# Alternating the products of two heads on TensorE, with shared PSUM tiles, in the four attentions of a two-layer block

## The chip, the cores and the metric

The kernel runs on one core of a Trainium2 chip. The metric is the device time of one execution in microseconds (us); a run of the kernel is a few such executions, and the median of them counts. A difference under 0.2% (about 2.2 us) can't be told from no change by such a measurement.

## The reference

Two transformer blocks over one sequence of 256 tokens, width 1024, all in float32. The first block has three branches that read the same normalised input: a pooling mixer, a stick-breaking attention with 8 heads of 64, and a cross attention with 4 heads of 64 over 256 memory rows. Their results are gated, merged, projected, and followed by a dense feed-forward layer. The second block has two causal attentions with 8 heads of 64 each (one of them with a top-64 selection of keys by an index score), gates, a projection, and a mixture of 32 experts with two experts per token.

```
# stick-breaking, per head:   z = q k^T / 8;  a = exp(logsig(z) + exclusive reverse cumsum(log1m));  out = a v
# cross, per head:            out = softmax(xq mk^T / 8) mv
# second block, per head:     out_a = softmax(causal(q k^T / 8)) v
#                             out_b = softmax(causal and top-64 by index score (q k^T / 8)) v
# then:  x = x + (sigmoid(ga) * (out_a w_a) + sigmoid(gb) * (out_b w_b)) w_out;   x = x + experts(x)
```

So there are four attentions: the stick-breaking one, the cross attention, and `attend` twice. In each of them the heads are worked through in pairs: 4 pairs, 2 pairs, and 4 pairs in each call of `attend`.

## The kernel before

Weights come from HBM as chunks of 1 MB on SyncE's queue, into rings of buffers. A chunk is split into a high part (ScalarE, L178, tiles `whi` or `wsw`) and a low part (VectorE, L179, `wlo` or `wsw`), and each dense product is three matmuls (`mm3`, L215 to L217). Dense products thus keep TensorE, ScalarE and VectorE busy together. The expert weights of the second block are used as they come.

The text of the kernel is not the order of the program. A list scheduler orders the instructions of each engine by its own estimate of when they are ready, and only `tc.issue_after` binds an order by hand. Around the attentions the dense products of the gates (tile `gate`) stand between the attention's products on TensorE, as filling.

Two heads of a pair lie on partitions 0 to 63 and 64 to 127. A score product contracts over 64 partitions, so head 0 uses the upper half of the array's rows and head 1 the lower half (shown as 64*128 in the trace). An output product contracts over all 128 and writes 64 partitions, so head 0 uses one half of the columns and head 1 the other (128*64). Every product in float32 appears as two matmul records.

The places that the change and the prediction touch:

- Stick-breaking (L534 to L565): scores `z` (L539, L541) into one tile of two PSUM banks, one bank per head; output `sbo` (L564).
- Cross attention (L570 on): scores `xs` (L576) into two tiles of one bank from the tag `m`; softmax; transposes `xpt` (L595) into another `m` tile per head; a copy `xpts` per head (L598, ScalarE); output `xob` (L605).
- `attend`, called for `b` and for `a` (L850 on): scores `as` (L860) into two tiles of one bank; maxima (L867, VectorE); exponentials (L874, ScalarE); reciprocal and scaling (L876, L880); three transposes per head back into the score's bank (L884); a copy `apts` per head (L886, ScalarE); output `ao` (L893).
- `acc_tile` hands out either a tile of two banks (pool `accp`, the first block up to the merge) or two tiles of one bank (pool `acc1`, four buffers, everything after). `ts_pair` uses it for the dense products with 512 columns: the two banks hold the two halves of the tokens. In the second block these are, in order, `qiT`, `qTb`, `kTb`, `vb`, `qTa`, `kTa`, `va`, ahead of `attend`'s score tiles.

What follows the attentions: the merge, the projection `wo2`, the routing, and eight groups of four experts, whose weights (201 MB) stream in on the same queue.

Of the kernel before, what the change touches and what calls it, by code (L numbers as in the profile page):

```python
# [18 lines left out]
P = 128  # L19
S = 256  # L20
# [61 lines left out]
def block_kernel(ctx: ExitStack, tc: tile.TileContext, A, out: bass.AP):  # L82
# [26 lines left out]
    def m_tile(n):  # L109
        return psum.tile([P, 512], F32, name=n, tag="m", bufs=2)  # L110
# [95 lines left out]
    def piece(v, a, b, after=(), eng=None):  # L206
        hi, lo = piece_tiles(a, b)
        with ExitStack() as q:
            for ins in after:
                q.enter_context(tc.issue_after(ins.ins))  # L210
            split_to(hi, lo, v, eng)
        return hi, lo

    def mm3(o, lh, rh, start, stop):
        nc.tensor.matmul(o, lhsT=lh[0], rhs=rh[0], start=start, stop=False)  # L215
# [318 lines left out]
    for hp in range(4):  # L534
        z = acc_tile("z")[2]
        zv = z[:, :, :384]
        for j in range(2):
            ks = slice(j * 64, j * 64 + 64)
            nc.tensor.matmul(z[:, j, 0:256], lhsT=kT[ks, hp, 0:P], rhs=qT[ks, hp, :], start=True, stop=True,  # L539
                             skip_group_check=True)  # L540
            nc.tensor.matmul(z[:, j, 256:384], lhsT=kT[ks, hp, P:S], rhs=qT[ks, hp, P:S], start=False, stop=True,  # L541
                             skip_group_check=True)
        e = tmp.tile([P, 2, 384], F32, name="se", tag="se", bufs=3)
        nc.scalar.activation(e, zv, AF.Abs)
        nc.scalar.activation(e, e, AF.Exp, scale=-1.0)
        nc.scalar.activation(e, e, AF.Ln, bias=1.0)
        nc.vector.scalar_tensor_tensor(out=e, in0=zv, scalar=0.0, in1=e, op0=ALU.max, op1=ALU.add)
        nc.vector.tensor_tensor(out=e, in0=e, in1=keep[:, None, :].to_broadcast([P, 2, 384]), op=ALU.mult)
        for j in range(2):
            nc.tensor.matmul(z[:, j, 0:256], lhsT=cst("tri"), rhs=e[:, j, 0:256], start=False, stop=True,  # L550
                             skip_group_check=True)
            nc.tensor.matmul(z[:, j, 128:256], lhsT=cst("one"), rhs=e[:, j, 256:384], start=False, stop=True,
                             skip_group_check=True)
            nc.tensor.matmul(z[:, j, 256:384], lhsT=cst("tri"), rhs=e[:, j, 256:384], start=False, stop=True,
                             skip_group_check=True)
        nc.vector.scalar_tensor_tensor(out=e, in0=zv, scalar=0.0, in1=drop[:, None, :].to_broadcast([P, 2, 384]),
                                       op0=ALU.min, op1=ALU.add)
        last_exp = nc.scalar.activation(e, e, AF.Exp)
        ob = m_tile("sbo")
        for k, c0, c1, a0 in ((0, 0, 256, 0), (1, 128, 256, 256)):  # L560
            for j in range(2):
                ps = slice(j * 64, j * 64 + 64)
                hc = slice((2 * hp + j) * 64, (2 * hp + j + 1) * 64)
                nc.tensor.matmul(ob[ps, c0:c1], lhsT=v[:, k, hc], rhs=e[:, j, a0:a0 + c1 - c0], start=(k == 0),  # L564
                                 stop=(k == 1), skip_group_check=True)  # L565
        split_to(sb[0][:, hp, :], sb[1][:, hp, :], ob[:, :S])


    xo = (mg1.tile([P, 2, S], F32R, name="xoh"), mg1.tile([P, 2, S], F32R, name="xol"))
    for hp in range(2):  # L570
        pts = []
        scs = [m_tile("xs").rearrange("p (t k) -> p t k", t=2) for j in range(2)]
        for tt in range(NT):
            for j in range(2):
                ks = slice(j * 64, j * 64 + 64)
                nc.tensor.matmul(scs[j][:, tt, :], lhsT=xqT[ks, hp, tt * P:(tt + 1) * P], rhs=mkT[ks, hp, :],  # L576
                                 start=True, stop=True, skip_group_check=True)
        for j in range(2):
            sc = scs[j]
            mx = tmp.tile([P, 2], F32, name="xmx", tag="xmx")  # L580
            nc.vector.tensor_reduce(out=mx, in_=sc, axis=AX.X, op=ALU.max, negate=True)
            pr = tmp.tile([P, 2, 256], F32, name="xp", tag="xp")
            sm = tmp.tile([P, 2], F32, name="xsm", tag="xsm")
            for tt in range(NT):
                nc.scalar.activation(pr[:, tt, :], sc[:, tt, :], AF.Exp, bias=mx[:, tt:tt + 1],
                                     accum_out=sm[:, tt:tt + 1])
            rc = tmp.tile([P, 2], F32, name="xrc", tag="xrc")
            nc.vector.reciprocal(rc, sm)
            for tt in range(NT):
                nc.vector.tensor_scalar(out=pr[:, tt, :], in0=pr[:, tt, :], scalar1=rc[:, tt:tt + 1],  # L590
                                        scalar2=None, op0=ALU.mult)
            pb = m_tile("xpt")
            for kt in range(2):
                for tt in range(NT):
                    nc.tensor.transpose(pb[:, kt * S + tt * P:kt * S + (tt + 1) * P],  # L595
                                        pr[:, tt, kt * P:(kt + 1) * P], ident)
            pt = tmp.tile([P, 2, S], F32, name="xpts", tag="xpts")
            nc.scalar.activation(pt.rearrange("p a s -> p (a s)"), pb, AF.Copy)  # L598
            pts.append(pt)
        ob = m_tile("xob")  # L600
        for kt in range(2):
            for j in range(2):
                ps = slice(j * 64, j * 64 + 64)
                hc = slice((2 * hp + j) * 64, (2 * hp + j + 1) * 64)
                nc.tensor.matmul(ob[ps, :S], lhsT=mv[:, kt, hc], rhs=pts[j][:, kt, :], start=(kt == 0),  # L605
                                 stop=(kt == 1), skip_group_check=True)
        split_to(xo[0][:, hp, :], xo[1][:, hp, :], ob[:, :S])


# [51 lines left out]

    ast.close()
    accp = None
    acc1 = ctx.enter_context(tc.tile_pool(name="acc1", bufs=4, space=PSUM, reuse_waits="tile"))
    accs = [acc_tile("wo") for _ in range(NT)]
    project("w_out", accs)
    s1.close()
# [121 lines left out]
        return dst  # L789


    qiT = rope_heads(3072, 1.0, "qiT", at, 4, first[0], 2)
    s1.close()
    homes.update(list=[base], i=0)
# [55 lines left out]
    def attend(qT, kT, v, bias, name):  # L850
        oh = (mg2.tile([P, 4, S], F32R, name=name + "h"), mg2.tile([P, 4, S], F32R, name=name + "l"))
        for hp in range(4):
            sc = acc_tile("as")
            st = tmp.tile([P, 16], F32, name="ast", tag="ast")
            mx, nm, sm, rc = (st[:, 4 * i:4 * i + 4] for i in range(4))
            prs, pts = [], []
            for j in range(2):
                ks = slice(j * 64, j * 64 + 64)
                for tt, a0, a1 in SPANS:
                    nc.tensor.matmul(sc[j][:, a0:a1], lhsT=qT[ks, hp, tt * P:(tt + 1) * P],  # L860
                                     rhs=kT[ks, hp, 0:a1 - a0], start=True, stop=True, skip_group_check=True)
            for j in range(2):
                pr = tmp.tile([P, 384], F32, name="ap", tag="ap", bufs=4)
                prs.append(pr)
                for tt, a0, a1 in SPANS:
                    c = 2 * j + tt
                    nc.vector.tensor_tensor_reduce(out=pr[:, a0:a1], in0=sc[j][:, a0:a1], in1=bias[:, a0:a1],  # L867
                                                   scale=1.0, scalar=GONE, op0=ALU.add, op1=ALU.max,
                                                   accum_out=mx[:, c:c + 1])
            nc.vector.tensor_scalar(out=nm, in0=mx, scalar1=-1.0, scalar2=None, op0=ALU.mult)  # L870
# [6 lines left out]
            for j in range(2):  # L877
                for tt, a0, a1 in SPANS:
                    c = 2 * j + tt
                    nc.vector.tensor_scalar(out=prs[j][:, a0:a1], in0=prs[j][:, a0:a1], scalar1=rc[:, c:c + 1],  # L880
                                            scalar2=None, op0=ALU.mult)
                pb = sc[j]
                for c in range(3):
                    nc.tensor.transpose(pb[:, c * P:(c + 1) * P], prs[j][:, c * P:(c + 1) * P], ident)  # L884
                pt = tmp.tile([P, 384], F32, name="apts", tag="apts")
                nc.scalar.activation(pt, pb[:, :384], AF.Copy)  # L886
                pts.append(pt)
            ob = m_tile("ao")
            for k, c0, c1, a0 in ((0, 0, 256, 0), (1, 128, 256, 256)):
                for j in range(2):  # L890
                    ps = slice(j * 64, j * 64 + 64)
                    hc = slice((2 * hp + j) * 64, (2 * hp + j + 1) * 64)
                    nc.tensor.matmul(ob[ps, c0:c1], lhsT=v[:, k, hc], rhs=pts[j][:, a0:a0 + c1 - c0], start=(k == 0),  # L893
                                     stop=(k == 1), skip_group_check=True)
            split_to(oh[0][:, hp, :], oh[1][:, hp, :], ob[:, :S])
        return oh

# [42 lines left out]
    for hf in range(2):  # L940
# [5 lines left out]
          for n, c in (("g", 1), ("s", 1), ("t", 1), ("u", 1), ("o", 2))}  # L946
    rings = [sw, (mgp, 2), (r3["g"], 1), (r3["s"], 1), (ring2r, 1), (ring2b, 2), (ring2, 3), (r3["t"], 1),
             (r3["u"], 1), (lows, 2), (r3["o"], 2), (ring, 4)]
    accs = [acc_tile("wo2") for _ in range(NT)]
    get = lambda kt: (mg, kt)  # L950
    for c in range(4):
# [433 lines left out]
```

## Time and profile before

| | |
|---|---|
| median of 3 runs | 1087.78 us (1086.56 to 1089.19) |
| the profiled execution's own time | 1086.86 us |
| its span, first to last instruction | 1085.1 us |
| TensorE busy | 953.6 us (88%) |
| VectorE busy | 451.3 us (42%) |
| ScalarE busy | 356.9 us (33%) |
| read from HBM | 308.20 MB, 285 GB/s over the span |
| chain that ended last | PE 62%, DMA 34% |

How to read it: the chain of work that ended last is followed back from the last instruction, at each step to what released it. It is TensorE's for the first two thirds of the span and the expert weights' DMA for the last third.

### The profile page before, as it was taken

The page shows a single profiled execution, that of the slowest core. Times are in us where ns is not written, and L with a number is a line of the kernel's source. Part 1 is how long each engine was busy: PE and PEld are TensorE (multiplying, and loading weights), DVE is VectorE, ACT ScalarE, POOL GpSimd, SP SyncE. Part 2 cuts the span into 40 slices and gives each one's busy share as a digit, 9 for nine tenths or more (in the row PEclk, how much of TensorE's full clock was granted, in tenths as well). Part 3 has the DMA queues.
Part 4 walks back from the last instruction along what each step waited for, and adds up shares of the span by engine and source line. Part 5 has one row for each costly group of instructions (what it writes and reads, how often), then busy time and mean ns, then how long its engine had stood idle before and what let it go on. Part 6 is the DMA issues. An engine that isn't in the chain of part 4 may idle for free.

```text
span 1085.1 us, 14832 instructions
## 1 busy us (share of the span) xinstructions
PE 953.6 (88%) x6159; PEld 654.4 (60%) x6159; DVE 451.3 (42%) x763; ACT 356.9 (33%) x564; POOL 50.2 (5%) x42
## 2 busy tenths in 40 slices
PE   7999999999999999999999999876776767667765
PEld 5989889978899996877889984312121212212111
DVE  4756538676545556679664751210101000101102
ACT  5645665455444443444665441000000000000002
POOL 2100013000000001212000000000000000000000
PEclk9999999999999999999999999987868887877878
DMA  8644336746555523745455789999999999999996
GB/s 336 251 156 154 129 113 261 270 181 247 190 178 185 198 96 127 301 153 179 171 170 228 291 328 408 419 418 419 417 421 416 419 416 422 417 421 420 417 421 273
DMA packets 50121, 310.28 MB, mean 286 GB/s; under 512 B 5504, under 2 KB 6656, under 8 KB 17920
## 3 DMA queue, kind: packets, MB, share of 16 engines
q1 hardware_dynamic: 49760, 309.19, 72.8%
q8 instruction: 50, 0.82, 0.3%
q14 instruction: 23, 0.19, 0.0%
q10 hardware_dynamic: 288, 0.08, 0.0%
HBM read 308.20 MB, written 1.05 MB: 285 GB/s over the span
## 4 chain that ended last, share of the span: by engine, by line
PE 62%; DMA 34%; DVE 2%; ACT 1%; issue 0%; SPq 0%; POOLq 0%; POOL 0%; ACTq 0%; DVEq 0%
DMA wchunk<-in_experts_dram 33%; PE gu L216 4%; PE gu L217 4%; PE gu L215 4%; PE gate L216 4%; PE gate L217 4%; PE gate L215 4%; PE hb L1242 3%; PE fo L216 2%; PE fo L215 2%; PE fo L217 2%; PE y L217 2%; PE y L215 2%; PE y L216 2%; PE wo L216 1%; PE wo L215 1%
## 5 line engine op out<-in xcount | busy, mean ns | idle before, releaser
L179 DVE TENSOR_TENSOR wlo<-wchunk,whi 128x1024 fp32r<-128x1024 f32 x146 | 182.8, 1257 | 112.8 <-ACT whi L178 109.7
L1242 PE MATMUL hb<-wchunk,xs 128*32 128x512 f32 x1016 | 160.6, 731 | 67.2 <-DMA wchunk<-in_experts_dram 63.5
L178 ACT ACTIVATE whi<-wchunk 128x1024 fp32r<-128x1024 f32 x151 | 156.7, 1048 | 167.0 <-PE gu L216 31.9
L1242 PEld LDWEIGHTS hb<-wchunk,xs 128*32 128x32 f32 x1016 | 26.2, 119 | 183.7 <-DMA wchunk<-in_experts_dram 143.6
L1242 PE MATMUL yb<-wchunk,mw 128*32 128x512 f32 (+1 forms) x544 | 74.6, 650 | 30.7 <-DMA wchunk<-in_experts_dram 27.7
L1306 DVE TENSOR_TENSOR x<-x,comb 128x512 f32<-128x512 f32 (+1 forms) x34 | 22.3, 656 | 141.8 <-PE comb L1304 141.6
L215 PE MATMUL gate<-xhi,whi 128*128 128x256 f32 x256 | 73.3, 286 | 0.0
L217 PE MATMUL gate<-xhi,wlo 128*128 128x256 f32 x256 | 73.2, 286 | 0.0
L216 PE MATMUL gate<-xlo,whi 128*128 128x256 f32 x256 | 73.0, 285 | 0.0
L1242 PEld LDWEIGHTS yb<-wchunk,mw 128*32 128x32 f32 x544 | 14.1, 116 | 84.6 <-DMA wchunk<-in_experts_dram 59.4
L179 DVE TENSOR_TENSOR wsw<-wchunk,wsw 128x1024 fp32r<-128x1024 f32 x35 | 43.1, 1231 | 35.6 <-ACT wsw L178 35.3
L1109 DVE TENSOR_TENSOR xs<-gat,gains 128x512 f32<-128x512 f32 x16 | 11.1, 691 | 111.9 <-PE gat L1101 111.9
L1269 ACT ACTIVATE mw<-hT 128x512 f32<-128x512 f32 x8 | 4.8, 597 | 153.2 <-PE hT L1267 153.2
L215 PE MATMUL gu<-xhi,whi 128*128 128x256 f32 x192 | 54.0, 281 | 0.0
L217 PE MATMUL gu<-xhi,wlo 128*128 128x256 f32 x192 | 54.0, 281 | 0.0
L216 PE MATMUL gu<-xlo,whi 128*128 128x256 f32 x192 | 53.9, 280 | 0.0
L1304 PE MATMUL comb<-ysb,mw 128*128 128x512 f32 (+1 forms) x68 | 43.6, 777 | 8.8 <-ACT ysb L1301 8.7
L178 ACT ACTIVATE wsw<-wchunk 128x1024 fp32r<-128x1024 f32 (+1 forms) x38 | 39.6, 1046 | 33.0 <-PE gu L217 11.0
L216 PEld LDWEIGHTS gate<-xlo,whi 128*128 128x128 f32 x256 | 48.3, 189 | 2.1 <-issue 1.8
L215 PEld LDWEIGHTS gate<-xhi,whi 128*128 128x128 f32 x256 | 48.4, 189 | 1.2 <-issue 1.2
L217 PEld LDWEIGHTS gate<-xhi,wlo 128*128 128x128 f32 x256 | 48.2, 188 | 1.4 <-issue 1.4
L1301 ACT ACTIVATE ysb<-yb 128x512 f32<-128x512 f32 (+1 forms) x17 | 9.7, 572 | 117.1 <-PE yb L1242 117.1
(483 smaller groups left out, 1986.6 us busy)
## 6 DMA issues: line engine op xcount, KB each, us to landing
wchunk<-in_experts_dram SPq DMA_DIRECT2D x187, 1024.0 KB, 19.8
wchunk<-in_dense_dram SPq DMA_DIRECT2D x92, 1024.0 KB, 4.9
wchunk<-in_experts_dram SPq DMA_DIRECT2D x8, 512.0 KB, 14.4
wchunk<-in_dense_dram SPq DMA_DIRECT2D x6, 512.0 KB, 6.6
memt<-in_mem_dram SPq DMA_DIRECT2D x2, 512.0 KB, 7.8
whalf<-in_experts_dram SPq DMA_DIRECT2D x2, 512.0 KB, 7.1
out_dram<-fo SPq DMA_DIRECT2D x2, 512.0 KB, 3.1
band<-in_bands_dram SPq DMA_DIRECT2D x2, 384.0 KB, 8.9
```

The source lines that it names most:

```text
L178: a = nc.scalar.activation(hi, src, AF.Copy)
L179: return a, (eng or nc.vector).tensor_tensor(out=lo, in0=src, in1=hi.bitcast(F32), op=ALU.subtract)
L215: nc.tensor.matmul(o, lhsT=lh[0], rhs=rh[0], start=start, stop=False)
L216: nc.tensor.matmul(o, lhsT=lh[0], rhs=rh[1], start=False, stop=False)
L217: return nc.tensor.matmul(o, lhsT=lh[1], rhs=rh[0], start=False, stop=stop)
L1109: nc.vector.tensor_tensor(out=xss[g][:, ks, :], in0=b.rearrange("p (k t) -> p k t", k=4), in1=gk[:, ks, None].to_broadcast([P, 4, P]), op= ...
L1242: nc.tensor.matmul(o[ps, :].rearrange("p (h n) -> p h n", h=m), lhsT=lhsT[:, ps], rhs=w[e], start=first, stop=last, skip_group_check=True, ...
L1269: nc.scalar.activation(mw[:, 1, :], b, AF.Copy)
L1301: nc.scalar.activation(y[:, cs], yb[:, :n], AF.Copy)
L1304: nc.tensor.matmul(cb[:, :n], lhsT=gT[:, tt * P:(tt + 1) * P], rhs=y[:, cs], start=True, stop=True)
L1306: nc.vector.tensor_tensor(out=xa, in0=xa, in1=cb[:, :n], op=ALU.add)
```

## The change

Three edits. (1) `in_turn` ties a list of products on TensorE one behind the other, and the score and output products of both heads are listed alternately, head 0, head 1, head 0, head 1. (2) Scores of both heads, and the transposed weights of both, share one tile of two PSUM banks, in the cross attention and in `attend` as they did in the stick-breaking one; the transposed weights of both heads are copied to SBUF by one ScalarE instruction instead of two. (3) For that, the second block up to the gates takes its `acc` tiles from a new pool `accp2` of two tiles of two banks, in place of four tiles of one bank; after it `acc3` has four of one bank again.

```diff
+    def in_turn(fns):
+        r = None
+        for fn in fns:
+            with ExitStack() as q:
+                if r is not None:
+                    q.enter_context(tc.issue_after(r.ins))
+                r = fn()
+        return r
...
-        scs = [m_tile("xs").rearrange("p (t k) -> p t k", t=2) for j in range(2)]
-        for tt in range(NT):
-            for j in range(2):
-                ks = slice(j * 64, j * 64 + 64)
-                nc.tensor.matmul(scs[j][:, tt, :], lhsT=xqT[ks, hp, tt * P:(tt + 1) * P], rhs=mkT[ks, hp, :],
-                                 start=True, stop=True, skip_group_check=True)
+        sc = acc_tile("xs")[2].rearrange("p j (t k) -> p j t k", t=2)
+        in_turn([lambda j=j, ks=slice(j * 64, j * 64 + 64), tt=tt: nc.tensor.matmul(
+            sc[:, j, tt, :], lhsT=xqT[ks, hp, tt * P:(tt + 1) * P], rhs=mkT[ks, hp, :], start=True, stop=True,
+            skip_group_check=True) for tt in range(NT) for j in range(2)])
...
-            pb = m_tile("xpt")
...
-            pt = tmp.tile([P, 2, S], F32, name="xpts", tag="xpts")
-            nc.scalar.activation(pt.rearrange("p a s -> p (a s)"), pb, AF.Copy)
-            pts.append(pt)
+        pt = tmp.tile([P, 2, 2, S], F32, name="xpts", tag="xpts", bufs=1)
+        nc.scalar.activation(pt, sc, AF.Copy)
...
+    acc1s.close()
+    ast = ExitStack()
+    accp = ast.enter_context(tc.tile_pool(name="accp2", bufs=2, space=PSUM, reuse_waits="tile"))
...
-            sc = acc_tile("as")
+            sc = acc_tile("as")[2]
...
-            for j in range(2):
-                ks = slice(j * 64, j * 64 + 64)
-                for tt, a0, a1 in SPANS:
-                    nc.tensor.matmul(sc[j][:, a0:a1], lhsT=qT[ks, hp, tt * P:(tt + 1) * P],
-                                     rhs=kT[ks, hp, 0:a1 - a0], start=True, stop=True, skip_group_check=True)
+            in_turn([lambda j=j, ks=slice(j * 64, j * 64 + 64), tt=tt, a0=a0, a1=a1: nc.tensor.matmul(
+                sc[:, j, a0:a1], lhsT=qT[ks, hp, tt * P:(tt + 1) * P], rhs=kT[ks, hp, 0:a1 - a0], start=True,
+                stop=True, skip_group_check=True) for tt, a0, a1 in SPANS for j in range(2)])
...
-                pt = tmp.tile([P, 384], F32, name="apts", tag="apts")
-                nc.scalar.activation(pt, pb[:, :384], AF.Copy)
-                pts.append(pt)
+            pt = tmp.tile([P, 2, 384], F32, name="apts", tag="apts", bufs=1)
+            nc.scalar.activation(pt, sc[:, :, :384], AF.Copy)
...
+            in_turn([lambda ps=slice(j * 64, j * 64 + 64), hc=slice((2 * hp + j) * 64, (2 * hp + j + 1) * 64), j=j,
+                     k=k, c0=c0, a0=a0: nc.tensor.matmul(ob[ps, c0:S], lhsT=v[:, k, hc], rhs=pt[:, j, a0:a0 + S - c0],
+                                                         start=(k == 0), stop=(k == 1), skip_group_check=True)
+                     for k, c0, a0 in ((0, 0, 0), (1, 128, 256)) for j in range(2)])
...
+    ast.close()
+    accp = None
+    acc1 = ctx.enter_context(tc.tile_pool(name="acc3", bufs=4, space=PSUM, reuse_waits="tile"))
```

The products of `z`, `sbo` and `xob` are tied in the same way. The scheduler makes a new order of it, in which three places matter here. The first is TensorE in the middle of `attend` for `b`, where the third pair's outputs meet the next pair's scores; `gate` is filling. Before:

```order
L217 MATMUL gate<-xhi,wlo 128x256
L893 MATMUL ao<-apts,vb 64x256
L860 MATMUL as<-kTb,qTb 128x128
L893 MATMUL ao<-apts,vb 64x256
L893 MATMUL ao<-apts,vb 64x128 x2
L860 MATMUL as<-kTb,qTb 128x256
L860 MATMUL as<-kTb,qTb 128x128
L860 MATMUL as<-kTb,qTb 128x256
L215 MATMUL gate<-xhi,whi 128x256
```

And now (line numbers are those of the changed kernel):

```order
L225 MATMUL gate<-xhi,whi 128x256
L887 MATMUL ao<-apts,vb 64x256 x2
L887 MATMUL ao<-apts,vb 64x128 x2
L858 MATMUL as<-kTb,qTb 128x128 x2
L858 MATMUL as<-kTb,qTb 128x256 x2
L226 MATMUL gate<-xlo,whi 128x256
```

The score product that stood between the two heads' outputs is behind them, and the two heads' scores stand next to each other.

The second place is TensorE at the scores of the cross attention's first pair. Before, the two products of one head stand behind the stick-breaking attention's last output, and those of the other head 22 gate products later:

```order
L564 MATMUL sbo<-se,v 64x256 x2
L564 MATMUL sbo<-se,v 64x128 x2
L576 MATMUL xs<-mkT,xqT 128x256 x2
L217 MATMUL gate<-xhi,wsw 128x256
L215 MATMUL gate<-xhi,wsw 128x256
```

Now all four products of the pair stand together, some 110 rows earlier, ahead of the third pair's output of the stick-breaking attention:

```order
L226 MATMUL gate<-xlo,whi 128x256
L577 MATMUL xs<-mkT,xqT 128x256 x4
L568 MATMUL sbo<-se,v 64x256 x2
L568 MATMUL sbo<-se,v 64x128 x2
L227 MATMUL gate<-xhi,wlo 128x256
```

The third place is VectorE where `vb` leaves PSUM (two halves of tokens) while the top-64 selection runs (`score`, `m8`); the same banks are the next ones for `qTa` on TensorE. Before, with buffer numbers (`vb_4610` and `vb_4611` are the two banks):

```order
L179 TENSOR_TENSOR wlo_4686<-wchunk_4683,whi_4701 128x1024
L905 COPY vb_4678<-vb_4610 128x512
L843 MATCH_REPLACE score_4317<-m8_4374,score_4317 128x128
L905 COPY vb_4678<-vb_4611 128x512
L767 TENSOR_TENSOR rr_4586<-kTb_4517,cs2_4154 128x512
```

Now both halves are of one tile, `vb_4601`:

```order
L179 TENSOR_TENSOR wlo_4675<-wchunk_4672,whi_4690 128x1024
L844 MATCH_REPLACE score_4310<-m8_4367,score_4310 128x128
L900 COPY vb_4668<-vb_4601 128x512
L843 MAX m8_4370<-score_4310 128x8
L900 COPY vb_4668<-vb_4601 128x512
L763 TENSOR_TENSOR rr_4577<-kTb_4509,cs2_4144 128x512
```

The two copies stand one instruction later in the queue, with a maximum between them, and the tile that `qTa` needs is free after the second of them. `qTa`'s first product waited for the first copy alone before.

## Rows read from the trace of the kernel before

**Rows 1.** The profile's page, its first line.

```profile
span 1085.1 us, 14832 instructions
```

**Rows 2.** Stretches: length, busy PE, PEld, DVE, ACT, POOL, granted clock, DMA share, GB/s.

```profile
128.00:165.00 37.00, 37.00 (x274) 32.69 (x273) 17.27 (x28) 24.54 (x47) 4.96 (x3) 1.00 0.36 128
...
511.00:586.00 75.00, 75.00 (x537) 61.96 (x536) 47.20 (x148) 46.10 (x113) 0.20 (x1) 1.00 0.45 158
...
610.00:650.00 40.00, 39.27 (x251) 34.14 (x253) 25.13 (x70) 17.48 (x29) 1.09 (x2) 1.00 0.91 353
...
700.00:800.00 100.00, 72.62 (x407) 19.34 (x404) 10.91 (x22) 4.78 (x8) 0.00 (x0) 0.78 1.02 419
```

**Rows 3.** The chain that ended last, in order of time: start, length, what.

```profile
694.21 19.89 DMA wchunk<-in_experts_dram
```

**Rows 4.** Waits of SyncE's queue: total us, times, longest.

```profile
SPq L161 <- DVE wlo L179: 333.0, 59, 13.1
```

**Rows 5.** The chain that ended last, stick-breaking attention.

```profile
75.31 0.64 PE z L539 x4
75.94 0.22 PE z L541 x4
...
127.31 0.80 PE sbo L564 x8
```

**Rows 6.** The same chain, cross attention.

```profile
128.11 1.06 PE xs L576 x4
...
139.73 0.57 PE xob L605 x2
...
143.97 1.01 PE xob L605 x6
```

**Rows 7.** The same chain, the two calls of attend.

```profile
522.10 0.85 PE as L860 x4
...
535.40 0.58 PE ao L893 x2
535.97 0.41 PE as L860 x2
536.39 0.79 PE ao L893 x5
537.18 0.86 PE as L860 x5
...
573.77 0.31 PE gate L216
```

**Rows 8.** Timeline of PE: start, length, instruction, idle time before it.

```profile
143.57 0.28 PE L215 MATMUL gate<-xhi,wsw 128*128 128x256 f32 x1
143.69 0.28 PE L216 MATMUL gate<-xlo,wsw 128*128 128x256 f32 x1
...
423.40 0.50 PE L215 MATMUL qiT<-wsw,xhi 128*128 128x512 f32 x1 [0.45 <-ACT xhi L178]
...
431.85 0.30 PE L345 MATMUL xtp<-ck,ntok 128*128 128x128 f32 x1 [1.27 <-DVE ntok L338]
...
481.39 0.50 PE L215 MATMUL qTa<-whi,xhi 128*128 128x512 f32 x1
```

**Rows 9.** Timeline of DVE.

```profile
423.03 0.68 DVE L356 TENSOR_TENSOR pn<-fo,grow 128x512 f32<-128x512 f32 x1
...
480.65 0.68 DVE L905 COPY vb<-vb 128x512 f32<-128x512 f32 x1
...
481.51 0.68 DVE L905 COPY vb<-vb 128x512 f32<-128x512 f32 x1
...
542.50 0.18 DVE L876 RECIPROCAL ast<-ast 128x4 f32<-128x4 f32 x1 [3.13 <-ACT ap L874]
```

**Rows 10.** Timeline of ACT.

```profile
111.93 0.79 ACT L544 ACTIVATE se<-z 128x768 f32<-128x768 f32 x1
...
539.85 0.87 ACT L886 ACTIVATE apts<-as 128x384 f32<-128x384 f32 x2 [2.25 <-PE as L884]
```

More of the change, by code (lines that the diff above doesn't have):

```diff
@@ L536, in block_kernel @@
         zv = z[:, :, :384]
-        for j in range(2):
-            ks = slice(j * 64, j * 64 + 64)
[L539 to L542, printed above, removed]
+        in_turn([lambda j=j, ks=slice(j * 64, j * 64 + 64), k0=k0, c0=c0, c1=c1: nc.tensor.matmul(
+            z[:, j, c0:c1], lhsT=kT[ks, hp, k0:k0 + P], rhs=qT[ks, hp, k0:S], start=(k0 == 0), stop=True,
+            skip_group_check=True) for k0, c0, c1 in ((0, 0, 256), (P, 256, 384)) for j in range(2)])
         e = tmp.tile([P, 2, 384], F32, name="se", tag="se", bufs=3)
@@ L559, in block_kernel @@
         ob = m_tile("sbo")
-        for k, c0, c1, a0 in ((0, 0, 256, 0), (1, 128, 256, 256)):
-            for j in range(2):
[L562 to L565, printed above, removed]
+        in_turn([lambda ps=slice(j * 64, j * 64 + 64), hc=slice((2 * hp + j) * 64, (2 * hp + j + 1) * 64), j=j, k=k,
+                 c0=c0, a0=a0: nc.tensor.matmul(ob[ps, c0:S], lhsT=v[:, k, hc], rhs=e[:, j, a0:a0 + S - c0],
+                                                start=(k == 0), stop=(k == 1), skip_group_check=True)
+                 for k, c0, a0 in ((0, 0, 0), (1, 128, 256)) for j in range(2)])
         split_to(sb[0][:, hp, :], sb[1][:, hp, :], ob[:, :S])
@@ L570, in block_kernel @@
     for hp in range(2):
-        pts = []
-        scs = [m_tile("xs").rearrange("p (t k) -> p t k", t=2) for j in range(2)]
-        for tt in range(NT):
-            for j in range(2):
-                ks = slice(j * 64, j * 64 + 64)
-                nc.tensor.matmul(scs[j][:, tt, :], lhsT=xqT[ks, hp, tt * P:(tt + 1) * P], rhs=mkT[ks, hp, :],
-                                 start=True, stop=True, skip_group_check=True)
+        sc = acc_tile("xs")[2].rearrange("p j (t k) -> p j t k", t=2)
+        in_turn([lambda j=j, ks=slice(j * 64, j * 64 + 64), tt=tt: nc.tensor.matmul(
+            sc[:, j, tt, :], lhsT=xqT[ks, hp, tt * P:(tt + 1) * P], rhs=mkT[ks, hp, :], start=True, stop=True,
+            skip_group_check=True) for tt in range(NT) for j in range(2)])
         for j in range(2):
-            sc = scs[j]
             mx = tmp.tile([P, 2], F32, name="xmx", tag="xmx")
-            nc.vector.tensor_reduce(out=mx, in_=sc, axis=AX.X, op=ALU.max, negate=True)
+            nc.vector.tensor_reduce(out=mx, in_=sc[:, j], axis=AX.X, op=ALU.max, negate=True)
             pr = tmp.tile([P, 2, 256], F32, name="xp", tag="xp")
@@ L584, in block_kernel @@
             for tt in range(NT):
-                nc.scalar.activation(pr[:, tt, :], sc[:, tt, :], AF.Exp, bias=mx[:, tt:tt + 1],
+                nc.scalar.activation(pr[:, tt, :], sc[:, j, tt, :], AF.Exp, bias=mx[:, tt:tt + 1],
                                      accum_out=sm[:, tt:tt + 1])
@@ L591, in block_kernel @@
                                         scalar2=None, op0=ALU.mult)
-            pb = m_tile("xpt")
             for kt in range(2):
                 for tt in range(NT):
-                    nc.tensor.transpose(pb[:, kt * S + tt * P:kt * S + (tt + 1) * P],
-                                        pr[:, tt, kt * P:(kt + 1) * P], ident)
-            pt = tmp.tile([P, 2, S], F32, name="xpts", tag="xpts")
-            nc.scalar.activation(pt.rearrange("p a s -> p (a s)"), pb, AF.Copy)
-            pts.append(pt)
-        ob = m_tile("xob")
[L601 to L606, printed above, removed]
+                    nc.tensor.transpose(sc[:, j, kt, tt * P:(tt + 1) * P], pr[:, tt, kt * P:(kt + 1) * P], ident)
+        pt = tmp.tile([P, 2, 2, S], F32, name="xpts", tag="xpts", bufs=1)
+        nc.scalar.activation(pt, sc, AF.Copy)
+        ob = m_tile("xob")
+        in_turn([lambda ps=slice(j * 64, j * 64 + 64), hc=slice((2 * hp + j) * 64, (2 * hp + j + 1) * 64), j=j, kt=kt:
+                 nc.tensor.matmul(ob[ps, :S], lhsT=mv[:, kt, hc], rhs=pt[:, j, kt, :], start=(kt == 0),
+                                  stop=(kt == 1), skip_group_check=True) for kt in range(2) for j in range(2)])
         split_to(xo[0][:, hp, :], xo[1][:, hp, :], ob[:, :S])
@@ L663, in block_kernel @@
     accp = None
-    acc1 = ctx.enter_context(tc.tile_pool(name="acc1", bufs=4, space=PSUM, reuse_waits="tile"))
+    acc1s = ExitStack()
+    acc1 = acc1s.enter_context(tc.tile_pool(name="acc1", bufs=4, space=PSUM, reuse_waits="tile"))
     accs = [acc_tile("wo") for _ in range(NT)]
@@ L852, in attend @@
         for hp in range(4):
-            sc = acc_tile("as")
+            sc = acc_tile("as")[2]
             st = tmp.tile([P, 16], F32, name="ast", tag="ast")
             mx, nm, sm, rc = (st[:, 4 * i:4 * i + 4] for i in range(4))
-            prs, pts = [], []
-            for j in range(2):
-                ks = slice(j * 64, j * 64 + 64)
-                for tt, a0, a1 in SPANS:
-                    nc.tensor.matmul(sc[j][:, a0:a1], lhsT=qT[ks, hp, tt * P:(tt + 1) * P],
-                                     rhs=kT[ks, hp, 0:a1 - a0], start=True, stop=True, skip_group_check=True)
+            prs = []
+            in_turn([lambda j=j, ks=slice(j * 64, j * 64 + 64), tt=tt, a0=a0, a1=a1: nc.tensor.matmul(
+                sc[:, j, a0:a1], lhsT=qT[ks, hp, tt * P:(tt + 1) * P], rhs=kT[ks, hp, 0:a1 - a0], start=True,
+                stop=True, skip_group_check=True) for tt, a0, a1 in SPANS for j in range(2)])
             for j in range(2):
@@ L866, in attend @@
                     c = 2 * j + tt
-                    nc.vector.tensor_tensor_reduce(out=pr[:, a0:a1], in0=sc[j][:, a0:a1], in1=bias[:, a0:a1],
+                    nc.vector.tensor_tensor_reduce(out=pr[:, a0:a1], in0=sc[:, j, a0:a1], in1=bias[:, a0:a1],
                                                    scale=1.0, scalar=GONE, op0=ALU.add, op1=ALU.max,
@@ L881, in attend @@
                                             scalar2=None, op0=ALU.mult)
-                pb = sc[j]
                 for c in range(3):
-                    nc.tensor.transpose(pb[:, c * P:(c + 1) * P], prs[j][:, c * P:(c + 1) * P], ident)
-                pt = tmp.tile([P, 384], F32, name="apts", tag="apts")
-                nc.scalar.activation(pt, pb[:, :384], AF.Copy)
-                pts.append(pt)
+                    nc.tensor.transpose(sc[:, j, c * P:(c + 1) * P], prs[j][:, c * P:(c + 1) * P], ident)
+            pt = tmp.tile([P, 2, 384], F32, name="apts", tag="apts", bufs=1)
+            nc.scalar.activation(pt, sc[:, :, :384], AF.Copy)
             ob = m_tile("ao")
[L889 to L894, printed above, removed]
+            in_turn([lambda ps=slice(j * 64, j * 64 + 64), hc=slice((2 * hp + j) * 64, (2 * hp + j + 1) * 64), j=j,
+                     k=k, c0=c0, a0=a0: nc.tensor.matmul(ob[ps, c0:S], lhsT=v[:, k, hc], rhs=pt[:, j, a0:a0 + S - c0],
+                                                         start=(k == 0), stop=(k == 1), skip_group_check=True)
+                     for k, c0, a0 in ((0, 0, 0), (1, 128, 256)) for j in range(2)])
             split_to(oh[0][:, hp, :], oh[1][:, hp, :], ob[:, :S])
```

## The prediction

> **What bounds the kernel now.** I read the page first: TensorE (PE) is busy for 88% of the span, and the chain that ended last is 62% PE and 34% DMA. An average over stages says little, so the stretches came next. In the first block's attentions, from 128 to 165 us, PE is busy in all of the 37.00 us, and in the second block's `attend`, from 511 to 586 us, in all of the 75.00 us, at full granted clock, with VectorE (DVE) at 47.20 and ScalarE (ACT) at 46.10 us [rows 2]. A busy PE is not a PE at its peak, so the attentions are bound by how many matmul records stand there and how close they follow each other. From 700 on it is another program: the DMA share is 1.02 at 419 GB/s, and PE is busy for only 72.62 of 100 us [rows 2].
>
> The tail decides whether time saved in the attentions is kept. The chain goes over to the expert weights at 694.21 us, with a piece of 19.89 us [rows 3]. If the weights streamed in regardless of PE, an earlier end of the attentions would meet an unchanged DMA. They don't: in 511 to 586 the DMA share is 0.45 [rows 2], and SyncE's queue of loads waits 333.0 us in all on `wlo`, the DVE instruction that frees a chunk's buffer [rows 4]. Dense products drive those splits, and PE drives the dense products. So the queue is held back by PE until the last dense weights are through (the share is 0.91 in 610 to 650 [rows 2]), and the tail should start earlier by what PE saves: one for one.
>
> **What alternating is worth.** The price of a pair whose heads run in both halves of the array at once is in the trace already. The stick-breaking scores take 0.64 + 0.22 = 0.86 us for both heads' 256 and 128 wide products, and its outputs 0.80 us for eight records [rows 5]. Since `z` has this price untied, its four pairs gain nothing, nor does `sbo`. The others:
>
> - `xs`: a head's products alone take 1.06 us [rows 6], and two pairs have four such blocks, 4.24 us. A tied pair is two 256-wide steps: 0.64 for the first, and twice the 0.22 that a step of half its width adds, 1.08 us. Gain 4.24 - 2.16 = 2.1 us.
> - `xob`: 0.57 for a first product alone, then 1.01 for six records [rows 6]. Paired, with eight records of which four are 256 wide instead of 128, it is `sbo`'s 0.80 and about 0.22. So 0.57 goes, twice: 1.1 us.
> - `as`: in the usual pair one product runs between the outputs (0.41) and the rest takes 0.86 [rows 7]; paired it is `z`'s 0.86. Seven of the eight pairs at 0.41, and one whose heads stood apart at 0.85 each [rows 7], which gains 0.84: 3.7 us.
> - `ao`: 0.58 + 0.79 [rows 7] becomes `sbo`'s 0.80. Gain 0.57, eight times: 4.6 us.
> - Lone gate products squeezed between the heads' outputs, in two places: 0.31 [rows 7] against a pace of 143.69 - 143.57 = 0.12 in the stream [rows 8]. Gain 0.4 us.
>
> The sum is 11.9 us. How sure is the step from the rows of `z` and `sbo` to `as` and `ao`? Shapes, type and halves of the array are the same, so the trace's own pair is the nearest row there is.
>
> The Trainium skill, "TensorE: Matmul & The Clock Gate", section "Part 3: Packing small matmuls — row/col tiling", says that matmuls start and end strictly in program order and only weight loads are pulled ahead. The program has `z` head by head. By that rule an untied `z` would cost more than a tied one; the records of 0.86 in all [rows 5], two heads' 256-wide ones and then two heads' 128-wide ones, speak against it, and it is a rival below.
>
> **What the change adds.**
>
> - *`qTa` behind both copies of `vb`.* `qTa`'s first product begins at 481.39, right after the first copy (480.65 + 0.68 = 481.33); the second ends at 481.51 + 0.68 = 482.19 [rows 8, 9]. Now both halves are one tile, so it waits for the second, and a maximum of the selection stands between the copies. The gap of 481.51 - 481.33 = 0.18 us held the `match_replace`, of the same width; I take that for the maximum. So 482.19 + 0.18 + 0.06 = 482.43, 1.0 us later, unless DVE itself comes earlier. Behind it on PE stands all of `qTa`; nothing fills. I take +1.0, bounds 0 and 1.2.
> - *`qiT`.* The new pool lies on banks that the projection before it read out last, so `qiT`'s first product also waits for `pn`, which ends at 423.03 + 0.68 = 423.71 instead of the 423.40 at which it starts now [rows 8, 9]: +0.3. In return the next normalisation's `ntok`, for which a transpose waits 1.27 at 431.85 [rows 8], goes ahead of a rotation on DVE and may come up to 0.6 earlier. I take 0, bounds a loss of 0.3 and a gain of 0.6.
> - *The other dense products* (`qTb`, `kTb`, `vb`, `kTa`, `va`, and `as` after them) get two-bank tiles in turn. In a pool of two tiles each waits for the one before last, which has been read some 3 us or more earlier by the order of DVE's copies. I take 0. If each of the seven handovers exposed what `qTa`'s does, it would be up to 7 us; a rival.
> - *One copy for two heads.* Two ACT copies of 0.87 become one, 768 wide. A copy-like instruction of that size from PSUM takes 0.79 [rows 10], so ACT saves nearly one copy. But the first head's outputs can't start before the whole is copied. Its price: `ao` starts later by up to 0.8 us for each pair, if PE has no other work. It has: some 28 gate products at 0.12 [rows 8], 3.4 us, stand between the last transposes and `ao`. I take 0, bounds 0 and 0.8 x 8 = 6.4.
> - *Common score tile.* The exponentials of the first head now wait for the second head's scores. These end within the same 0.86, so nothing is lost; and ACT idles 2.25 us before the copies, DVE 3.13 before the reciprocal [rows 9, 10], so the softmax chain has room.
>
> **Sum.** -11.9 + 1.0 = -10.9 us. The profiled execution took 1086.86 us, 1.8 above its span [rows 1] and 0.9 below the median of 1087.78; I expect 1075.96 for a profiled one, and **1076.9 us** for the median.
>
> **The rivals.**
>
> *Half of it.* The handovers of two-bank tiles, seven times about 1 us as at `qTa` with six more, and none of the gain lost otherwise: -10.9 + 6 = -4.9, about 1082.9. The same result comes from the other side if the shorter loop runs into the softmax chain: PE's loop is 542.62 - 535.33 = about 7.3 us for a pair now, shortened by 1.0, and if the chain (the common tile, the exponentials, the scaling, the copy) takes 0.8 more than that in each pair, the 6.4 above is lost: -4.5. For it: PE waits on DVE for the first time in the places above. Against it: the idle times of 2.25 and 3.13 [rows 9, 10]. Bounds 1079.8 to 1085.5.
>
> *Nothing moves.* Either the queue of expert weights is bound by the DMA before 694 and the saved time turns into waiting at the first expert, or the untied heads already run beside each other, as `z` does, in a way that the grouping in [rows 7] hides. For the first: the share of 0.91 in 610 to 650. Against it: 0.45 in 511 to 586, and the 333 us for which the loads wait [rows 2, 4]. Time: 1087.8.
>
> *Slower.* The softmax chain becomes the bound in every pair of `attend`. The exponentials, the maxima, the scaling and the copy of a pair are one chain now, as both heads begin with one tile and end with one copy. To lose, each of eight pairs must wait (10.9 + 2.2) / 8 = 1.6 us beyond what fills PE. For that ACT's 2.25 of slack, less the 1.0 by which the loop shrinks, and the gate products between (3.4 us) must both be used up. At 1.9 us for each pair it is -10.9 + 15.2 = +4.3, 1092. Against it: ACT's merged copy gives back about 0.9.
>
> *Matmuls strictly in order.* If PE takes no product ahead of another, the untied `z`, which the program has as 256, 128, 256, 128, can't have run in pairs, and tying it saves one score product's 0.41 [rows 7] in each of its four pairs, 1.6 more: 1075.3. The 0.86 of [rows 5] leaves little of that. It is what the rule of the Trainium skill above would give.
>
> **How the numbers follow.** The full forecast, between -14 and -8 (1073.8 to 1079.8): 0.60, the strict-order case 0.03 within it. Half: 0.28. Nothing moves: 0.07. Slower: 0.05. A difference of 0.2%, 2.2 us, is what a measurement can tell from none. Nearly all of "half" lies more than 2.2 under the present time, so faster is 0.60 + 0.27 = 0.87, the same 0.08, slower 0.05. The range: from the gain of 11.9 with nothing lost and the bounds of `ntok` and `z` on top, 0.6 and 1.6 (1087.8 - 14.1 = 1073.7, rounded to 1073.5), to the worse part of "half", 1083.5. Outside it lie "nothing", "slower" and a quarter of "half", 0.19. The likeliest case's own range is 1073.8 to 1079.8.
>
> **What would show it.** In the profile after: `as` and `ao` as blocks of 0.86 and 0.80 us for both heads, `xs` as one block of eight records near 1.07, and PE still busy in all of the two windows that now end earlier; the chain's first expert piece near 683 instead of 694; `qTa` waiting for DVE for about 1 us. Idle PE ahead of the transposes or `ao` would show "half" or "slower"; blocks of the size above with the expert piece still at 694 would show that the DMA held the end. Blocks that are no shorter would make the prediction wrong at its root.

## The result, and the profile after

The changed kernel takes 1074.47 us (median of 4 runs, 1072.31 to 1076.47), the kernel before 1087.70 (median of 4, one run more than in the table of the section on time before): ratio 0.9878, 95% interval 0.9866 to 0.9890, so 12.0 to 14.6 us faster. The forecast was 1076.9 us, 10.9 faster.

The page of the changed kernel begins with its span, 14.5 us under that of [rows 1]:

```profile
span 1070.6 us, 14816 instructions
```

The stretches of the changed kernel (columns as in [rows 2]): the first two lie around the attentions, the third in the experts.

```profile
127.00:160.00 33.00, 33.00 (x278) 31.43 (x275) 16.66 (x24) 23.65 (x41) 4.95 (x3) 1.00 0.48 176
507.00:572.00 65.00, 65.00 (x534) 57.88 (x534) 44.84 (x144) 43.51 (x105) 0.00 (x0) 1.00 0.50 182
700.00:800.00 100.00, 70.91 (x424) 19.76 (x426) 11.05 (x22) 3.58 (x6) 0.00 (x0) 0.83 1.02 419
```

TensorE (PE) is still busy in every microsecond of the attentions. They are shorter because fewer of those microseconds hold one head alone. The chain of the changed kernel shows it, in the places of [rows 5, 6, 7]:

```profile
74.30 0.85 PE z L547 x8
...
112.49 1.06 PE xs L577 x8
...
133.34 1.01 PE xob L600 x8
...
530.03 0.80 PE ao L887 x8
530.83 0.86 PE as L858 x8
...
630.76 1.16 PE gat L1099 x8
...
679.50 19.89 DMA wchunk<-in_experts_dram
```

An `xs` block of eight records for two heads is as long as one of four records for one head was, 1.06 us. `xob` has lost its lone product of 0.57, `ao` its lone one of 0.58, and nothing stands between `ao` and `as` any more. `z` has its old price.

PE's timeline of the changed kernel, where the prediction looked for new waits (compare [rows 8]):

```profile
418.87 0.47 PE L225 MATMUL qiT<-wsw,xhi 128*128 128x512 f32 x1 [0.90 <-ACT xhi L178]
...
426.27 1.29 PE L355 MATMUL xtp<-ck,ntok 128*128 128x128 f32 x8 [0.68 <-DVE ntok L348]
...
476.60 0.50 PE L225 MATMUL qTa<-whi,xhi 128*128 128x512 f32 x1 [0.75 <-DVE vb L900]
```

and VectorE's (DVE), with the two copies of `vb` and the maximum between them (compare [rows 9]):

```profile
475.08 0.68 DVE L900 COPY vb<-vb 128x512 f32<-128x512 f32 x1
475.67 0.28 DVE L843 MAX8 m<-score 128x8 f32<-128x128 f32 x1
475.88 0.67 DVE L900 COPY vb<-vb 128x512 f32<-128x512 f32 x1
```

**Three stretches.** Runs of one kernel differ by up to 4 us. Between two fixed instructions of PE there is much less scatter, as the table below shows. So I cut each profiled span at two places: the last `qk` product, ahead of the attentions, and the first `gat` product, which opens the experts. In the two kernels these are, on PE's timeline (the kernel before first):

```profile
55.36 0.28 PE L217 MATMUL qk<-xhi,wsw 128*128 128x256 f32 x1
...
645.20 1.05 PE L1101 MATMUL gat<-pm,nt 128*128 128x128 f32 x7 [0.73 <-DVE pm L1096]
```

```profile
54.36 0.28 PE L227 MATMUL qk<-xhi,wsw 128*128 128x256 f32 x1
...
630.76 1.16 PE L1099 MATMUL gat<-pm,nt 128*128 128x128 f32 x8 [0.72 <-DVE pm L1094]
```

The middle stretch goes from 645.20 - 55.36 = 589.84 to 630.76 - 54.36 = 576.40 us: 13.44 less. The rest behind `gat` is 1085.1 - 645.2 = 439.9 us before and 1070.6 - 630.8 = 439.8 after, so the tail took over the whole gain. The first stretch is 1.00 us shorter. The same for all kernels of this study:

| kernel | median us | ratio to before (95%) | to last `qk` | `qk` to `gat` | behind `gat` |
|---|---|---|---|---|---|
| before | 1087.70 | 1 | 55.36 | 589.84 | 439.9 |
| changed | 1074.47 | 0.9878 (0.9866 to 0.9890) | 54.36 | 576.40 | 439.8 |
| tiles_only | 1074.42 | 0.9876 (0.9861 to 0.9891) | 54.82 | 576.41 | 441.5 |
| ties_only | 1088.54 | 1.0004 (0.9996 to 1.0013) | 55.18 | 590.59 | 441.1 |
| by_head | 1074.82 | 0.9877 (0.9861 to 0.9892) | 55.18 | 576.49 | 442.5 |
| two_copies | 1082.56 | 0.9953 (0.9940 to 0.9966) | 55.24 | 584.05 | 439.8 |
| head1_first | 1082.52 | 0.9958 (0.9944 to 0.9972) | 55.08 | 584.21 | 439.9 |
| late_pool | 1073.58 | 0.9876 (0.9861 to 0.9891) | 55.29 | 576.10 | 439.9 |
| cross_only | 1083.82 | 0.9966 (0.9954 to 0.9978) | 55.47 | 585.81 | 440.0 |
| attend_only | 1078.86 | 0.9918 (0.9905 to 0.9932) | 55.27 | 580.34 | 441.4 |
| turned_together | 1073.51 | 0.9880 (0.9860 to 0.9899) | 55.74 | 576.21 | 440.0 |

Each ratio is to runs of the kernel before on the same chip as its own, so it isn't exactly that of the medians shown. The last three columns come from one profiled execution each. The first stretch varies from 54.36 to 55.74 between kernels that hardly differ there, and the tail from 439.8 to 442.5. So the 1.00 us of the first stretch is scatter, not the change; the middle, which agrees within 0.1 us in changed, tiles_only and by_head, is what the edits can be read from.

### The profile page after: what moved, and what is told of

It reads as the page before. It is cut to its first block, busy times and chain, and to the rows that moved or that the text cites. A ratio compares the mean times of both kernels' runs of the same rounds, so it can differ in the third digit from the quotient of the medians.

```text
span 1070.6 us, 14816 instructions
## 1 busy us (share of the span) xinstructions
PE 935.4 (87%) x6159; PEld 648.8 (61%) x6159; DVE 451.2 (42%) x763; ACT 354.8 (33%) x554; POOL 50.4 (5%) x42
## 4 chain that ended last, share of the span: by engine, by line
PE 60%; DMA 36%; DVE 2%; ACT 1%; issue 0%; SPq 0%; POOL 0%; POOLq 0%; ACTq 0%; DVEq 0%
DMA wchunk<-in_experts_dram 35%; PE gu L226 4%; PE gu L227 4%; PE gu L225 4%; PE gate L227 4%; PE gate L226 4%; PE gate L225 4%; PE hb L1240 3%; PE fo L226 2%; PE fo L225 2%; PE fo L227 2%; PE y L227 2%; PE y L225 2%; PE y L226 2%; DMA wchunk<-in_dense_dram 1%; PE gat L1099 1%
## 5 line engine op out<-in xcount | busy, mean ns | idle before, releaser
L178 ACT ACTIVATE whi<-wchunk 128x1024 fp32r<-128x1024 f32 (+1 forms) x151 | 156.7, 1048 | 162.9 <-PE gu L226 31.9
L1302 PE MATMUL comb<-ysb,mw 128*128 128x512 f32 (+1 forms) x68 | 38.4, 695 | 9.2 <-ACT ysb L1299 9.2
```

Source lines behind the costliest of these rows:

```text
L178: a = nc.scalar.activation(hi, src, AF.Copy)
L1302: nc.tensor.matmul(cb[:, :n], lhsT=gT[:, tt * P:(tt + 1) * P], rhs=y[:, cs], start=True, stop=True)
```

## The experiments

**tiles_only**: is it the ties? The changed kernel, with `in_turn` no longer binding anything:

```diff
         for fn in fns:
             with ExitStack() as q:
-                if r is not None:
-                    q.enter_context(tc.issue_after(r.ins))
                 r = fn()
```

> The changed kernel with the ties taken out: the products are listed alternately and the tiles and the copy are shared, but nothing binds their order on TensorE. Theory (a shared tile and a shared copy make all products of a pair ready at once, and the scheduler then puts them next to each other by itself): as and ao stay blocks of 0.86 and 0.80 us, and the time is that of the changed kernel, 1074.5 us, within 1.5. Rival (the ties make the gain): the blocks fall apart into 0.58 + 0.41 + 0.79 + 0.86 again, and the time goes back to 1084 to 1088.

The middle stretch is 576.41 us against 576.40, the median 1074.42. The chain:

```profile
524.19 0.80 PE ao L885 x8
524.99 0.85 PE as L856 x8
```

In this kernel the ties contribute nothing. With one tile for both heads and one copy, the products, still listed alternately in the text, become ready together, and the scheduler sets them side by side without being bound to.

**ties_only**: the other half alone. The kernel before, with all lists of products tied alternately, but two score tiles, two copies and the old pools:

```diff
-            for j in range(2):
-                ks = slice(j * 64, j * 64 + 64)
-                for tt, a0, a1 in SPANS:
-                    nc.tensor.matmul(sc[j][:, a0:a1], ...
+            in_turn([lambda j=j, ...: nc.tensor.matmul(sc[j][:, a0:a1], ...
+                for tt, a0, a1 in SPANS for j in range(2)])
```

> The kernel before with the ties alone: every head keeps its own score tile and its own copy, the pools are as before. Theory (readiness decides, a tie cannot make the second head ready earlier): the first product of a pair still starts alone as soon as its own tile or copy is there, so as, ao, xs and xob gain little: 1085.5 to 1088 us, against 1087.7 before. Rival (ties are enough): nearly the whole gain without the later start of qTa, 1073.5 to 1077 us.

1088.54 us, no gain; the middle is even 0.75 longer. The chain has the pattern of [rows 7] again:

```profile
528.27 0.57 PE ao L887 x2
528.85 0.41 PE as L856 x2
529.26 0.79 PE ao L887 x5
530.06 0.85 PE as L856 x4
```

The first output goes out alone after the first copy, and a score product fills the time until the second. A tie says what comes first; it can't keep the first one back until the second is ready.

**by_head**: does the order within a pair count? The changed kernel with the lists in another order:

```diff
-                stop=True, skip_group_check=True) for tt, a0, a1 in SPANS for j in range(2)])
+                stop=True, skip_group_check=True) for j in range(2) for tt, a0, a1 in SPANS])
```

(and so for `z`, `sbo`, `xs`, `xob` and `ao`).

> The changed kernel, with the products of a pair tied in another order: all of head 0, then all of head 1, side by side in the program but not alternating. Theory (TensorE runs neighbours in different halves of the array beside each other, as z of the kernel before did with this order at 0.86 us for a pair): blocks of the same length, 1074.5 us within 1.5. Rival (only strict alternation pairs them): each of the 28 pairs loses 0.2 to 0.6 us, 1080 to 1088 us.

1074.82 us, the middle 576.49, and in the chain:

```profile
530.87 0.81 PE ao L887 x8
531.67 0.86 PE as L858 x8
```

So the products needn't alternate; they have to be neighbours. Head 0's two products and then head 1's two take what the alternating order takes.

**two_copies**: what the one copy does. The changed kernel with

```diff
-            nc.scalar.activation(pt, sc[:, :, :384], AF.Copy)
+            for j in range(2):
+                nc.scalar.activation(pt[:, j], sc[:, j, :384], AF.Copy)
```

and the same in the cross attention.

> The changed kernel with the transposed weights of each head copied by an instruction of its own, into the same tile; ties and shared score tiles stay. Theory (the one copy is what brings the outputs of both heads together): as and xs keep their 0.86 and 1.06, but the first output product starts alone after the first copy, 0.57 us more in each of 8 ao pairs and 2 xob pairs: 5 to 6 us more than the changed kernel, 1079 to 1081 us. Rival (the one copy is neutral, as the prediction had it in its sum): 1074.5 us within 1.5.

1082.56 us; the middle is 7.65 longer than with one copy, more than the 5 to 6 expected. The chain says why:

```profile
532.89 0.58 PE ao L889 x2
533.47 0.31 PE gate L227
533.78 0.80 PE ao L889 x5
534.58 0.85 PE as L859 x8
```

Beside the lone 0.58 there is a gate product that takes 0.31 instead of the stream's 0.12 [rows 8]: (0.57 + 0.19) x 10 pairs = 7.6. The scores, with their common tile, keep their 0.85. The middle is still 5.79 shorter than before; that is what is left to the shared score tiles and the new pool.

**head1_first**: can pairs be had without sharing? `ties_only`, with each list of the cross attention and of `attend` beginning with the head whose copy comes last:

```diff
-                     for k, c0, a0 in ((0, 0, 0), (1, 128, 256)) for j in range(2)])
+                     for k, c0, a0 in ((0, 0, 0), (1, 128, 256)) for j in (1, 0)])
```

> The kernel before with the ties alone (each head its own score tile and its own copy), but in the cross attention and in attend each tied list begins with head 1, whose copy comes last. Theory (what counts is that all products of a pair are ready when the first one starts; sharing is only one way to it): ao and xob come together without a shared copy, 0.57 us in each of 8 and 2 pairs, 5.7 us; as and xs, whose two tiles come free apart, still start with a lone product: 1082 us within 1.5. Rival (the shared tile and copy themselves make the gain): no gain, 1086.5 to 1088.5 us.

1082.52 us, the middle 5.63 shorter than before. Its chain has whole `ao` blocks, from two copies and a tie, and lone scores:

```profile
533.66 0.42 PE as L856 x2
534.08 0.32 PE gate L225
534.39 0.80 PE ao L887 x8
535.19 0.85 PE as L856 x4
```

Readiness decides, then, and a shared copy is one way to it. A tie is another, if it holds the early head behind the late one.

**cross_only** and **attend_only**: do the parts add? The kernel before with the edit of the cross attention alone, and with those of `attend` and the pools alone (diffs as in the section on the change, each with its own places only, ties included).

> The kernel before with the edit of the cross attention alone (shared score tile, one copy, ties). Theory (the parts add, and the tail moves with PE one for one): xs 2.1, xob 1.1 and some 0.4 us of transposes and gate products, 3.6 us: 1084.1 us within 1.2, and the expert weights' first bound piece begins as much earlier. Rival (a small gain early in the program is lost again before the tail, where loads or other waits set the pace): 1086.5 to 1088 us.

> The kernel before with the edit of attend and of the pools alone; the first block is as before. Theory (the parts add): 9.5 us in attend, less 0.8 at qTa and with 0.5 from the earlier ntok, 9.2 us: 1078.5 us within 1.5. Rival (the two parts share one slack, so that either alone gives most of the gain): 1074.5 to 1076.5 us.

1083.82 and 1078.86 us. The middle stretches are 4.03 and 9.50 us shorter; together 13.53, against 13.44 for the whole. They add, and the early gain of the cross attention is neither lost nor absorbed over the 480 us that lie between it and the experts. The first expert piece that I named as a marker is a poor one: in cross_only the chain goes over to DMA at

```profile
667.87 19.96 DMA wchunk<-in_experts_dram
```

26 us earlier than in [rows 3], while the first `gat` product moves by only 3.92. In the eleven profiles of the table it lies anywhere between 661.08 (turned_together) and 694.21, without following the time.

**late_pool**: is there a version without the late `qTa`? The changed kernel with the pool opened ahead of `attend`, so that `qiT` to `va` keep single banks:

```diff
-    acc1s.close()
-    ast = ExitStack()
-    accp = ast.enter_context(tc.tile_pool(name="accp2", bufs=2, space=PSUM, reuse_waits="tile"))
     qiT = rope_heads(3072, 1.0, "qiT", at, 4, first[0], 2)
...
+    acc1s.close()
+    ast = ExitStack()
+    accp = ast.enter_context(tc.tile_pool(name="accp2", bufs=2, space=PSUM, reuse_waits="tile"))
     outs = {name: attend(*qkv[name], bias, "o" + name) for name, bias in (("b", sbias), ("a", cneg))}
```

> The changed kernel with the pool of two-bank tiles opened just ahead of attend, so that the dense products of the second block keep single banks. Theory (the pool costs the start of qTa 0.8 us and the start of qiT 0.45 us, and nothing else): qTa starts right behind the first copy of vb again, 0.8 to 1.3 us less than the changed kernel, 1073.2 to 1073.7 us. Rival (the change of pool only moves: attend's first two-bank tile must now wait for the last single banks, va's, and the order around it changes): 1074.5 to 1077 us, with PE idle or as later at the start of attend.

The middle is 576.10 us, 0.30 less; the median 1073.58 can't be told from the changed kernel's. `qTa` has no idle time ahead of it any more, but the transposes ahead of `qiT`'s second part wait 1.27 for `ntok` again, as in [rows 8]:

```profile
427.76 1.29 PE L355 MATMUL xtp<-ck,ntok 128*128 128x128 f32 x8 [1.27 <-DVE ntok L348]
...
477.28 0.50 PE L225 MATMUL qTa<-whi,xhi 128*128 128x512 f32 x1
```

The pool's two prices (at `qiT` and `qTa`) and its gain at `ntok` nearly cancel. The theory had left out the gain, and the rival's late start of `attend` did not come.

**turned_together**: does the rule hold for transposes? `late_pool` with all transposes of a pair tied, head 1 in front:

```diff
+            in_turn([lambda j=j, c=c: nc.tensor.transpose(sc[:, j, c * P:(c + 1) * P], prs[j][:, c * P:(c + 1) * P],
+                                                          ident) for j in (1, 0) for c in range(3)])
```

> The kernel with the late pool, and with all transposes of a pair (six in attend, eight in the cross attention) tied with head 1, which is ready last, in front. Theory (what holds for the products holds for the transposes: a group that starts with a lone one loses a little at each end): some 0.1 us at each of a dozen breaks, 1.2 us less than with the late pool, 1072 to 1073 us; in the trace the last gate product comes about 1 us earlier after the first qk product than with the late pool. Rival (a broken group of transposes costs nothing, as they use the whole array like the gate products between them): the distance from the first qk product to the last gate product is the same within 0.3 us, and the time is 1073.6 us within 1.

The middle is 576.21 us against 576.10: the theory was wrong. A broken group of transposes costs nothing that can be seen here. In late_pool's chain transposes and the gate product between them keep their own pace, 0.11 and 0.12 each:

```profile
525.04 0.11 PE as L877
525.15 0.12 PE gate L225
525.27 0.33 PE as L877 x3
```

and six of them together, in the chain of this run, take the same 0.11 each:

```profile
527.54 0.66 PE as L878 x6
```

## Why the prediction was right, and where its sum fell short

The mechanism was as predicted: attentions bound by PE, a lone head's block as long as that of both heads, a tail that moves one for one. The forecast of 10.9 was too small all the same. Term by term, over the middle stretch of 13.44 us:

- `xs`: forecast 2.1, and two blocks of 1.06 in place of four: 2.1. `xob`: forecast 1.1, measured 2 x 0.57. `ao`: forecast 4.6; 0.58 + 0.79 against 0.80 in eight pairs: 4.6. `z` and `sbo`: forecast nothing; `z` 0.86 before and 0.85 now, `sbo` 0.80 in both.
- `as`: forecast 3.7, measured 3.9. The first pair had more of a lone product in it than the 0.41 that I took for it, 0.85 + 0.62 in the chain before:

```profile
511.55 0.85 PE as L860 x6
...
512.98 0.62 PE as L860 x2
```

- `qTa`: forecast +1.0; the last `vb` product came 5.59 us earlier than before and `qTa`'s first one 4.79, so +0.8. The mechanism is in the rows above: 0.75 idle, released by the second copy, 475.88 + 0.67 = 476.55.
- `qiT` and `ntok`: forecast 0 with bounds of a loss of 0.3 and a gain of 0.6. The idle time ahead of `qiT` grew from 0.45 to 0.90, that ahead of the transposes fell from 1.27 to 0.68, and the stage as a whole (from the last `fo` product to the last `vb` product) got 0.6 shorter. That this is the bound on the gain is in part luck. PE's idle time in the stage fell by only 0.3 (2.2 to 1.9), and what gave the other 0.3 isn't shown; in late_pool, without the new pool there, the stage is as long as before. Nor was it `pn` that ended `qiT`'s wait, as the prediction had it with 0.3: `pn` ended at 418.04 + 0.68 = 418.72, the second half of `xhi` at 417.78 + 1.07 = 418.85, and `qiT` starts at 418.87.

```profile
417.78 1.07 ACT L178 ACTIVATE xhi<-xtp 128x512 fp32r<-128x512 f32 x2
...
418.04 0.68 DVE L366 TENSOR_TENSOR pn<-fo,grow 128x512 f32<-128x512 f32 x1
```

- Gate products beside blocks, forecast 0.4 for two places: this is the term that was mis-sized, and the transposes had no term at all. The price is not one of lone gate products. From one start to the next, a gate product ahead of a half-array block takes 0.21 and one behind it 0.22, in place of 0.12. On the timeline of before:

```profile
535.12 0.28 PE L217 MATMUL gate<-xhi,wlo 128*128 128x256 f32 x1
535.33 0.65 PE L893 MATMUL ao<-apts,vb 128*64 128x256 f32 x2
...
537.97 0.39 PE L215 MATMUL gate<-xhi,whi 128*128 128x256 f32 x1
538.19 0.27 PE L216 MATMUL gate<-xlo,whi 128*128 128x256 f32 x1
```

  A transpose beside such a block pays too: 0.20 ahead of one and 0.16 behind it, in place of 0.11. (Behind a transpose a gate product shows 0.20 too, but the transpose ahead of it shows 0.03, so that border costs nothing.) Counted over the middle stretch there were 33 separate runs of half-array products before and are 23 now, so there are ten fewer pairs of borders. All gate products together took 120.2 us before and 119.2 after, 1.0 less; the transposes 1.5 in the cross attention and 4.3 in `attend` before, 1.2 and 3.9 after, 0.7 less. The excess at the borders, over both, fell from 4.8 to 3.1, which is nearly all of it.

Together: 1.3 for borders (1.0 + 0.7 - 0.4), 0.6 for the stage of `qiT` and `ntok`, 0.2 each for `as` and `qTa`, 2.3 of the missing 13.44 - 10.9 = 2.5.

Two steps were right for the wrong reason. The section on alternating speaks of a tied pair, but tiles_only and ties_only show that in this order the ties do nothing and the common readiness does all. And the one copy stood in the sum with 0, as a cost that gate products hide. Hidden it is (PE has no idle time in 65.00 us), but without it 7.65 us of the 13.44 would not have come: two_copies shows that, with head 0 listed first, it is the edit that brings the outputs together. Whoever had split the change by this sum would have kept the ties and dropped the copy.

Of the rivals, the half gain fell with the handovers: one of seven (`qTa`) is to be seen in PE's idle times, and `qiT` by 0.45. The bound in the softmax chain did not come: no idle PE at all in the stretch. The tail followed, which settles the case in which nothing moves. The strict order of matmuls is refuted: `z` takes 0.85 tied and 0.86 untied, and by_head runs every pair by head at no loss. The Trainium skill, "TensorE: Matmul & The Clock Gate", section "Part 3: Packing small matmuls — row/col tiling", has matmuls start and end in program order. In by_head the pair of outputs is bound as head 0's 256 and 128 wide products, then head 1's. Its trace has two 256-wide records 0.013 us apart and the first 128-wide one 0.48 us behind them. A record doesn't name its head, but the two records of one product alone start 0.27 us apart, so one of the two must be of head 1's product, third in the program; the trace decides here.

## What to carry to other kernels

Half-array score products of two heads cost what one head's cost here (0.86 against 0.85, 1.06 against 1.06), provided both are ready when the first is issued, and two heads' outputs pair in the same way. Look in the chain for a lone block of half the records, and ask what makes its partner late: another tile to come free, another copy to end. Make that event one for both (one tile, one copy), or hold the early one behind the late one; binding the order early one first gives nothing. A merged copy that looks like pure delay can be the edit that pays, as long as other work fills the engine that waits for it.

## What was not expected of the hardware

TensorE paired two heads whose products were not alternating: 0.81 us for a pair of outputs listed head by head, 0.80 alternately. And it is the border between full-array and half-array products that costs, some 0.1 us on each side of a block, whether the block holds one head or two; a full-array product alone between two blocks pays both, 0.31 us in place of 0.12. Between transposes and gate products, both 128*128, no such price is seen.
